# Pooling branch: its gates computed in pairs before the pooling, groups in reverse order, maps one group behind, weight splits by adding DMAs, early products reordered

## The chip, the cores and the metric

The kernel runs on one core of one Trainium2 chip. The metric is the device time of one launch in microseconds (us); three runs before the change gave 894.7, 896.02 and 897.62 us, median 896.02. Engines are named as in the profile: PE (TensorE, matrix products), PEld (its weight loads), DVE (VectorE), ACT (ScalarE), POOL (GpSimd) and SP (SyncE, which issues most DMAs).

## The reference, cut to what matters

One decoder layer on 512 prompt tokens and 64 sample tokens (576 in all), model width 1024, fp32:

```python
xn = rms_norm(h, g_mix[i])
z = xn @ w_in[i]
b, c, hc = z[..., :o1], z[..., o1:o2], z[..., o2:o3]
v = z[..., o3:o4]
gate_a = jax.nn.sigmoid(z[..., o4:o5])
gate_b = jax.nn.sigmoid(z[..., o5:])
ya, cb = gated_short_conv(b, c, hc, conv_bufs[i], w_conv[i])
ya = ya @ w_out_conv[i]
yb, pb = multiscale_pool(v, pool_bufs[i], pos0, w_pool[i], pool_scale[i])
h = h + (gate_a * ya + gate_b * yb) @ w_o[i]
```

`multiscale_pool` takes four groups of 256 channels; in each, the mean over the last 2, 4, 8 or 16 tokens minus the token itself, then a 256x256 map of the group and a scale per channel. A squared-ReLU feed-forward part (1024 to 4096 and back), a per-layer input embedding and a last norm follow. `w_in` has six parts of 1024 output channels: b, c, hc, v, gate a, gate b.

## The kernel before, in words

Channels lie on the 128 partitions, tokens on the free axis in two halves of 288 (256 prompt and 32 sample tokens each). Every fp32 operand of a product is split into a rounded `hi` and a rest `lo` (`split`, L87: ACT writes hi, DVE writes lo = source - hi), and a product is three matmuls per weight block: hi with hi, hi with lo, lo with hi (`mm`, L104). A product of 128 output channels over 1024 input channels (`product`, L118) is 8 x 3 x 2 = 48 matmuls of 288 columns.

Some products are done in pairs of output blocks with a Strassen-like form (`pairs_of`, L416): seven quarter products of 12 matmuls instead of eight, with sums of weights (`Form`, L157, partly added up by DMAs that POOL issues, L154) and sums of activations (`Operand`, L378; `differences`, L407). This is how gate a, most of b's neighbours c and hc, and the feed-forward part's first matrix are computed; gate b and v use plain products. In `pairs_of` a flag `late` holds back the last quarter of the inner index of the first four quarter products.

Weights come through one `Stream` (L180): an ordered list of parts of 128x512, loaded by SP into 8 raw buffers and split some parts ahead into 7 buffers of hi and of lo (`wsp`).

The stages up to the place where the change ends are:
1. Opening: eight input blocks are scaled and split while three plain products (c, hc, b of block 0) run over k = 0 to 7 (L486); the token sums of squares for the norm (`Rms.tokens`, 18 narrow fp32 matmuls, L329) come after k = 5, and the spreading of the norm factors to all partitions (`spread`, L347) after k = 6. `copies` (L352) brings the factors to SBUF as r1 and its square r1s; only then can the products be scaled (L558) and their six PSUM banks be given back.
2. Convolution branch (L553 to L598): block 4 by plain products, then q = 1 to 3 in pairs. The sums of activations for the pairs are made inside the loop over j at L564 to L569.
3. Gate a in pairs (L616), four pairs.
4. The map of the convolution branch, `w_oc` (L630), eight products, multiplied into gate a (`mix`).
5. Pooling (L636 to L694): per group two products of v (L640), running sums on DVE (L657), the pooled difference split (L677), two products for gate b with a sigmoid (L680 to L685), and the group's map (L689) that is scaled, gated and added to mix (L691, L693) and split into `merged`.
6. The output matrix `w_o` (L715): two products are opened together, over the first six blocks of merged first, then the last two (`two_products`, L370).

The compiler's scheduler orders each engine's instructions by priority in program order; where `pinned` is set PE keeps program order (L65).

## Time and profile before

| | |
|---|---|
| median of three runs | 896.02 us |
| the profiled execution | 897.59 us |
| its span, first to last instruction | 895.8 us |
| mean granted TensorE clock, share of full | 0.988 |
| PE busy in the span | 878.8 us, 98% |
| DVE busy | 581.2 us, 65% |
| ACT busy | 405.0 us, 45% |
| POOL busy | 131.1 us, 15% |

PE is busy nearly always, and the chain that ended last runs through it for 94% of the span. Such a busy PE still hides two things: matmuls run at half rate where the granted clock is at the lower of its two levels, and short waits add up. So the reading goes by stages: where PE starts late, how long one matmul takes there, and what it waited for.

### The profile page before, as it was taken

How to read it: one execution, taken by the hardware profiler on the slowest of the kernel's cores; microseconds unless marked ns; L12 is line 12 of the kernel's file. 1: busy time of each engine (PE TensorE's matmuls, PEld its weight loads, DVE VectorE, ACT ScalarE, POOL GpSimd, SP SyncE). 2: the span in 40 equal slices, each digit the busy share in tenths (PEclk: the TensorE clock that was granted, in tenths of full speed). 3: DMA queues.
4: the chain of work that ended last, by engine and by line, in shares of the span. 5: the costliest groups of instructions: out<-in, count | busy, mean ns of one | idle time of the engine just before them, and what ended most of it. 6: DMA issues, size and time to landing. Idle time of an engine off the chain costs nothing.

```text
span 895.8 us, 16709 instructions
## 1 busy us (share of the span) xinstructions
PE 878.8 (98%) x6554; PEld 875.5 (98%) x6554; DVE 581.2 (65%) x1027; ACT 405.0 (45%) x702; POOL 131.1 (15%) x168
## 2 busy tenths in 40 slices
PE   9989999999999999999999999999999999999995
PEld 9979999999999999999999999999999999999995
DVE  7886887985336677767884347534773367687455
ACT  7643443553113333345774237522672157536432
POOL 4101111100001221022110100011000110021354
PEclk9889999999999999999999999999999999999998
DMA  7526455554222222363553535353543544332002
GB/s 258 133 81 145 140 128 149 139 147 140 83 83 83 83 83 83 114 194 92 134 155 104 133 97 137 121 130 101 154 133 87 124 122 130 104 97 94 14 16 91
DMA packets 58125, 103.88 MB, mean 116 GB/s; under 512 B 6848, under 2 KB 10560, under 8 KB 58048
## 3 DMA queue, kind: packets, MB, share of 16 engines
q1 hardware_dynamic: 50416, 89.16, 31.0%
q0 software_dynamic: 7488, 13.63, 9.7%
q8 instruction: 51, 0.84, 0.4%
q14 instruction: 26, 0.21, 0.1%
q10 hardware_dynamic: 144, 0.03, 0.0%
HBM read 99.82 MB, written 2.99 MB: 115 GB/s over the span
## 4 chain that ended last, share of the span: by engine, by line
PE 94%; DVE 3%; DMA 1%; ACT 1%; issue 1%; SPq 0%; DVEq 0%
PE b L67 68%; PE ps L67 18%; PE psg L67 6%; DVE lo L94 1%; PE psn L329 1%; PE psn L347 1%; DMA raw<-w_up 1%; DMA xin<-x 0%; ACT hi L93 0%; DVE xall L808 0%; DVE t L691 0%; DVE gt L409 0%; ACT hi L96 0%; DVE gt L412 0%; DVE gt L411 0%
## 5 line engine op out<-in xcount | busy, mean ns | idle before, releaser
L67 PE MATMUL b<-hi 128*128 128x288 f32 x1592 | 403.1, 298 | 5.2 <-ACT hi L93 3.6
L67 PE MATMUL b<-lo,hi 128*128 128x288 f32 x1592 | 402.1, 297 | 0.7 <-DVE lo L94 0.7
L67 PE MATMUL b<-hi,lo 128*128 128x288 f32 x1592 | 402.1, 297 | 0.4 <-DVE lo L94 0.4
L93 ACT CAST hi<-raw 128x512 fp32r<-128x512 f32 x300 | 184.6, 620 | 323.6 <-PE b L67 214.6
L67 PEld LDWEIGHTS b<-hi 128*128 128x128 f32 x1592 | 278.0, 190 | 6.8 <-ACT hi L93 4.3
L94 DVE TENSOR_TENSOR lo<-raw,hi 128x512 fp32r<-128x512 f32 x300 | 210.6, 707 | 112.0 <-ACT hi L93 108.9
L67 PEld LDWEIGHTS b<-lo,hi 128*128 128x128 f32 x1592 | 278.1, 190 | 1.3 <-DVE lo L94 1.2
L67 PEld LDWEIGHTS b<-hi,lo 128*128 128x128 f32 x1592 | 277.7, 190 | 0.7 <-DVE lo L94 0.7
L67 PE MATMUL ps<-hi 128*128 128x288 f32 x416 | 89.2, 296 | 0.0
L67 PE MATMUL ps<-hi,lo 128*128 128x288 f32 x416 | 89.1, 296 | 0.0
L67 PE MATMUL ps<-lo,hi 128*128 128x288 f32 x416 | 89.1, 296 | 0.0
L154 POOL DMA_DIRECT2D raw<-w_up x32 | 27.7, 865 | 327.6 <-DMA raw<-w_up 188.8
L67 PEld LDWEIGHTS ps<-hi,lo 128*128 128x128 f32 x416 | 67.0, 189 | 0.0
L67 PEld LDWEIGHTS ps<-lo,hi 128*128 128x128 f32 x416 | 67.0, 189 | 0.0
L67 PEld LDWEIGHTS ps<-hi 128*128 128x128 f32 x416 | 67.0, 189 | 0.0
L320 POOL TENSOR_TENSOR sq<-sq 128x576 f32<-128x576 f32 (+2 forms) x32 | 41.2, 1286 | 112.3 <-ACT sq L314 64.6
L174 DVE TENSOR_TENSOR s<-raw 128x512 f32<-128x512 f32 x26 | 17.9, 690 | 49.3 <-DMA raw<-w_up 32.5
L93 ACT CAST hi<-s 128x512 fp32r<-128x512 f32 x52 | 32.0, 617 | 38.1 <-PE b L67 33.0
L94 DVE TENSOR_TENSOR lo<-s,hi 128x512 fp32r<-128x512 f32 x52 | 35.7, 687 | 13.1 <-ACT hi L93 12.1
L67 PE MATMUL psg<-hi 128*128 128x320 f32 (+1 forms) x128 | 38.2, 298 | 0.7 <-ACT r L354 0.7
L67 PE MATMUL psg<-lo,hi 128*128 128x320 f32 (+1 forms) x128 | 37.9, 296 | 0.0
L67 PE MATMUL psg<-hi,lo 128*128 128x320 f32 (+1 forms) x128 | 37.9, 296 | 0.0
(130 smaller groups left out, 751.0 us busy)
## 6 DMA issues: line engine op xcount, KB each, us to landing
raw<-w_in SPq DMA_DIRECT2D x100, 256.0 KB, 2.9
raw<-w_up SPq DMA_DIRECT2D x80, 256.0 KB, 2.9
raw<-w_down SPq DMA_DIRECT2D x64, 256.0 KB, 2.9
raw<-w_up POOLq DMA_DIRECT2D x32, 256.0 KB, 4.4
raw<-w_in POOLq DMA_DIRECT2D x20, 256.0 KB, 4.9
raw<-w_oc SPq DMA_DIRECT2D x16, 256.0 KB, 2.8
raw<-w_o SPq DMA_DIRECT2D x16, 256.0 KB, 2.8
raw<-w_pg SPq DMA_DIRECT2D x16, 256.0 KB, 2.8
```

The source lines that it names most:

```text
L67: i = nc.tensor.matmul(*args, **kw)
L93: nc.scalar.copy(hi, src)
L94: nc.vector.tensor_tensor(out=lo, in0=src, in1=as32(hi), op=ALU.subtract)
L154: nc.gpsimd.dma_start(raw, y, accum_op=ALU.add)
L174: nc.vector.tensor_tensor(out=p.rs2, in0=p.rs1, in1=p.ra, op=ALU.add)
L320: nc.gpsimd.tensor_tensor(out=self.parts[0], in0=self.parts[0], in1=sq, op=ALU.add)
L329: nc.tensor.matmul(sums[:, i:i + 1], a[:, h, c:c + m], ones32[:, 0:1], start=k == 0, stop=k == len(self.parts) - 1)
L347: nc.tensor.matmul(self.ps[:, h, c:c + m], self.y[:, i:i + 1].broadcast_to([m, P]), idt[:m, :m], start=True, stop=True)
```

## The change

Five things are done.

- Opening (L505 and on, new): the sums of squares are issued in three portions of six, each behind one of the three products of k = 5; then the remaining k = 6 and 7 are done product by product, and the spreading is issued in two halves inside the second product.
- Convolution branch: a function `differences(k)` makes the activation sums, called once before the convolution of a block and once before its last product's gate; the first pair (q = 1) uses `late`.
- Gate b is computed in pairs, with the same functions as gate a, after the `w_oc` products and before the pooling. The `w_oc` products come before the scope of pools changes. Gate b's eight tiles live in the `acts` pool.
- Pooling: groups go from window 16 to window 2, a group's map (`merge`) is issued behind the next group's two products, and small copies go from POOL to ACT. The weights of v of the last three groups and of all maps are "adding" parts: ACT writes hi, then lo = -hi, and a DMA issued by POOL adds the weight from HBM onto lo; DVE does not touch them.
- The first two `w_o` products go over merged blocks 2 to 7 first, then 0 and 1, and two PSUM pools change places.

```diff
         def split(self):
+            if self.adding:
+
+                n = self.ap.shape[1]
+                hi = wsp.tile([P, KH], F32R, tag="w", name="hi")[:, :n]
+                lo = wsp.tile([P, KH], F32R, tag="wl", name="lo")[:, :n]
+                nc.scalar.copy(hi, self.raw[:, :n])
+                nc.scalar.mul(lo, as32(hi), -1.0)
+                nc.gpsimd.dma_start(lo, self.ap, accum_op=ALU.add)
+                self.raw = None
+                return hi, lo
...
-    for g in range(4):
+    order += forms([Pair(w_in[5 * NJ + q], w_in[5 * NJ + NQ + q]) for q in range(NQ)])
+    for g in (3, 2, 1, 0, -1):
         for i in range(2):
-            order += unit(w_in[3 * NJ + 2 * g + i])
-        for i in range(2):
-            order += unit(w_in[5 * NJ + 2 * g + i])
-        order += unit(w_pool[g])
+            order += unit(w_in[3 * NJ + 2 * g + i], g < 3) if g >= 0 else []
+        order += unit(w_pool[g + 1], True) if g < 3 else []
...
-    for k in range(NJ):
+    def first_step(k, u):
+        mm(both(ps0[u]), [first[k]], u * P, P, xg[k], k == 0, k == NJ - 1)
+
+    for k in range(NJ - 2):
         for u in range(3):
-            mm(both(ps0[u]), [first[k]], u * P, P, xg[k], k == 0, k == NJ - 1)
-        if k == 5:
-            stat.tokens()
-        if k == 6:
-            r1, r1s = stat.copies(stat.spread(), "r", "rs")
+            first_step(k, u)
+            if k == NJ - 3:
+                stat.sums((2 * u, 2 * u + 1))
+    stat.tokens(summed=True)
+    for u in range(3):
+        for k in (NJ - 2, NJ - 1):
+            first_step(k, u)
+            if u == 1:
+                r = stat.spread(range(3 * (k - NJ + 2), 3 * (k - NJ + 3)))
+    r1, r1s = stat.copies(r, "r", "rs")
...
+        differences(j // 2)
         conv.convolve()
-        conv.gate(ps0[2] if j == 0 else product(stream.take(2), xg))
-        for k in range(j // 2, j // 2 + 2):
-            g = tmp.tile([P, 4, HT], F32, tag="g", name="gx", bufs=2)
-            for i in range(2):
-                nc.scalar.mul(g[:, 2 * i:2 * i + 2], xs[k + i * NQ], v(G_MIX, k + i * NQ))
-            xo.differences(k, g)
+        ps_b = ps0[2] if j == 0 else product(stream.take(2), xg)
+        differences(j // 2 + 1)
+        conv.gate(ps_b)
...
-        pairs_of(2, xo, corner, finish, filler=filler)
+        pairs_of(2, xo, corner, finish, q == 1, filler=filler)
...
+    gates, where, tag = mix, keep, "keep"
+    pairs_of(NQ, xo, corner, finish)
+    for j in range(NJ):
+        ps = product(stream.take(2), ya_in)
+        for h in range(NH):
+            nc.vector.tensor_tensor(out=mix[j][:, h], in0=ps[h], in1=mix[j][:, h], op=ALU.mult)
+    ya_in = None
+    gates, where, tag = [None] * NJ, acts, "act"
     pairs_of(NQ, xo, corner, finish)
...
+    def merge(g, pooled):
+        wp = stream.take()
+        for i in range(2):
+            j = 2 * g + i
+            ps = product(wp, pooled, base=i * P, step=2 * P)
...
+    before = None
+    for g, w in reversed(list(enumerate(WINDOWS))):
...
-        gates = []
-        for i in range(2):
-            ps = product(stream.take(2), xg)
-            z = tmp.tile([P, NH, HT], F32, tag="t", name="zb")
-            nc.vector.tensor_tensor(out=z, in0=halves(ps), in1=r1, op=ALU.mult)
...
+        if before:
+            merge(*before)
+        before = g, pooled
+    merge(*before)
...
-    opened = two_products(merged, range(NJ))
+    opened = two_products(merged, [*range(2, NJ), 0, 1])
```

How the built programs differ is shown at three places. The first is PE in the opening, from the last two products of k = 5 to the spreading; `psn<-ones,sq` are the sums of squares, `psn<-idt,ry` the spreading, and each L67 row is a step of the three products. Before:

```order
L67 MATMUL b<-hi,lo 128x288 x2
L329 MATMUL psn<-ones_121,sq 96x1 x18
L67 MATMUL b<-hi 128x288 x2
...
L67 MATMUL b<-hi,lo 128x288
L347 MATMUL psn<-idt,ry 128x96 x6
L67 MATMUL b<-hi,lo 128x288
L67 MATMUL b<-hi 128x288 x2
```

After:

```order
L340 MATMUL psn<-ones_121,sq 96x1 x6
L67 MATMUL b<-hi 128x288 x2
L67 MATMUL b<-lo,hi 128x288 x2
L67 MATMUL b<-hi,lo 128x288 x2
L340 MATMUL psn<-ones_121,sq 96x1 x6
...
L340 MATMUL psn<-ones_121,sq 96x1 x6
...
L367 MATMUL psn<-idt,ry 128x96 x3
L67 MATMUL b<-hi,lo 128x288
L367 MATMUL psn<-idt,ry 128x96 x3
L67 MATMUL b<-hi 128x288 x2
```

One run of 18 narrow matmuls became three of 6 with six wide matmuls between them (PE runs each fp32 one in two passes, so that the trace shows 36). The spreading stands 23 wide matmuls behind the last sum in both, now in two halves with one wide matmul between, and the whole third product follows it.

The second place is DVE before the first pair of the convolution branch. `gt` and the `lo` made from it are the activation sums of k = 3, `bt` is the gated convolution of block 4, `b` in its source the product it waits for. Before:

```order
L542 TENSOR_TENSOR bt_717<-b_668,r_407 128x288
L94 TENSOR_TENSOR lo_763<-raw_581,hi_762 128x512
L543 TENSOR_TENSOR bt_717<-bt_717,cv_652 128x2x256
L546 TENSOR_TENSOR bt_717<-bt_717,cv_652 128x2x32
L94 TENSOR_TENSOR lo_789<-s2_583,hi_788 128x512
L94 TENSOR_TENSOR lo_723<-bt_717,hi_722 128x576
L94 TENSOR_TENSOR lo_738<-gt_729,hi_737 128x576
L409 TENSOR_TENSOR gt_744<-gx_741 128x576
L411 TENSOR_TENSOR gt_744<-gx_741,gt_744 128x288
L412 TENSOR_TENSOR gt_744<-gx_741,gt_744 128x288
L94 TENSOR_TENSOR lo_749<-gt_744,hi_748 128x576
L94 TENSOR_TENSOR lo_753<-gt_744,hi_752 128x576
```

After:

```order
L429 TENSOR_TENSOR gt_735<-gx_732 128x576
L94 TENSOR_TENSOR lo_757<-raw_522,hi_756 128x512
L431 TENSOR_TENSOR gt_735<-gx_732,gt_735 128x288
L94 TENSOR_TENSOR lo_740<-gt_735,hi_739 128x576
L432 TENSOR_TENSOR gt_735<-gx_732,gt_735 128x288
L570 TENSOR_TENSOR bt_747<-b_682,r_425 128x288
L570 TENSOR_TENSOR bt_747<-b_683,r_425 128x288
L94 TENSOR_TENSOR lo_744<-gt_735,hi_743 128x576
L571 TENSOR_TENSOR bt_747<-bt_747,cv_667 128x2x256
L574 TENSOR_TENSOR bt_747<-bt_747,cv_667 128x2x32
```

The sums of k = 3 stood behind the whole gated convolution; now they stand ahead of it, except for one split.

The third place is PE from the last map of the pooling (group 0, weights `hi_4377`) to the first `w_o` product (`b_4708`), after the change. `hi_4572` and `lo_4573` are the pooled block 1, `hi_4604`/`lo_4605` and `hi_4624`/`lo_4625` are merged blocks 2 and 3, which come from the map issued just before:

```order
L67 MATMUL ps_4654<-hi_4492,lo_4378 128x288 x2
L67 MATMUL ps_4634<-hi_4572,hi_4377 128x288 x2
L67 MATMUL ps_4654<-hi_4572,hi_4377 128x288 x2
L67 MATMUL ps_4634<-lo_4573,hi_4377 128x288 x2
...
L67 MATMUL b_4708<-hi_4604,hi_4424 128x288
...
L67 MATMUL b_4708<-lo_4605,hi_4424 128x288
...
L67 MATMUL b_4708<-hi_4624,hi_4424 128x288
...
L67 MATMUL b_4708<-lo_4625,hi_4424 128x288
...
L67 MATMUL b_4708<-hi_4398,hi_4498 128x288
```

And DVE's own order over the same stretch, after the change (`t` are the merged blocks before their split, `lo_4631` a `w_o` weight):

```order
L94 TENSOR_TENSOR lo_4573<-pl_4566,hi_4572 128x576
L681 TENSOR_TENSOR t_4601<-t_4601,ga_2502 128x576
L681 TENSOR_TENSOR t_4621<-t_4621,ga_2649 128x576
L94 TENSOR_TENSOR lo_4631<-raw_4422,hi_4630 128x512
L94 TENSOR_TENSOR lo_4605<-t_4601,hi_4604 128x576
L679 SCALAR_TENSOR_TENSOR t_4647<-ps_4634,vec_82,ga_3309 128x576
L94 TENSOR_TENSOR lo_4625<-t_4621,hi_4624 128x576
```

Before the change the `w_o` products began with merged blocks 0 to 5, finished two groups earlier; now blocks 2 and 3 come first, right behind the group that makes them.

## Rows read from the trace of the kernel before

**Rows 1.** The page: busy time of each engine in the span, and the chain that ended last by engine.

```profile
PE 878.8 (98%) x6554; PEld 875.5 (98%) x6554; DVE 581.2 (65%) x1027; ACT 405.0 (45%) x702; POOL 131.1 (15%) x168
...
PE 94%; DVE 3%; DMA 1%; ACT 1%; issue 1%; SPq 0%; DVEq 0%
```

**Rows 2.** Busy time in stretches: stretch and its length, then busy us (instructions) of PE, PEld, DVE, ACT and POOL, granted TensorE clock as a share of 2.4 GHz, DMA share, GB/s.

```profile
21.60:25.00 3.40, 3.40 (x38) 3.40 (x36) 2.64 (x5) 1.96 (x2) 0.59 (x1) 0.87 0.75 214
25.00:30.60 5.60, 5.60 (x24) 5.60 (x25) 5.05 (x13) 4.34 (x8) 1.31 (x2) 0.50 0.75 172
...
55.40:60.00 4.60, 1.17 (x5) 0.63 (x4) 4.43 (x8) 2.58 (x5) 0.00 (x0) 0.81 0.17 57
60.00:65.00 5.00, 4.82 (x19) 4.50 (x20) 2.93 (x6) 1.34 (x3) 0.00 (x0) 0.50 0.00 0
...
440.00:454.00 14.00, 12.88 (x97) 12.48 (x96) 11.43 (x18) 9.51 (x17) 4.85 (x4) 1.00 0.56 136
...
821.90:823.00 1.10, 1.10 (x15) 1.10 (x14) 0.77 (x2) 0.76 (x4) 0.00 (x0) 1.00 0.46 168
```

**Rows 3.** PE in order of time in the opening: start, us, engine, line, operation, count, in brackets the idle time before and its releaser.

```profile
21.56 3.55 PE L329 MATMUL psn<-ones,sq 128*96 128x1 f32 x36
...
30.64 1.62 PE L347 MATMUL psn<-idt,ry 96*128 96x96 f32 x12
...
34.09 0.40 PE L67 MATMUL b<-hi 128*128 128x288 f32 x1
```

**Rows 4.** DVE in order of time in the opening and before the first pair, same columns.

```profile
8.09 0.55 DVE L94 TENSOR_TENSOR lo<-fraw,hi 128x384 fp32r<-128x384 f32 x1
...
10.48 1.79 DVE L94 TENSOR_TENSOR lo<-fraw,hi 128x384 fp32r<-128x384 f32 x1
...
27.31 0.15 DVE L340 SCALAR_TENSOR_TENSOR ry<-rz,ry 96x6 f32<-96x6 f32 x1
27.57 0.76 DVE L94 TENSOR_TENSOR lo<-gt,hi 128x576 fp32r<-128x576 f32 x1
...
33.58 0.82 DVE L558 TENSOR_TENSOR c<-b,rs 128x288 f32<-128x288 f32 x2 [2.94 <-ACT rs L358]
...
57.36 0.76 DVE L409 TENSOR_TENSOR gt<-gx 128x576 f32<-128x576 f32 x1
```

**Rows 5.** ACT in order of time, same columns.

```profile
32.29 0.64 ACT L354 COPY r<-psn 128x576 f32<-128x576 f32 x1 [2.48 <-PE psn L347]
32.83 0.66 ACT L358 ACTIVATE rs<-psn 128x576 f32<-128x576 f32 x1
...
59.71 0.39 ACT L421 COPY g<-b 128x288 f32<-128x288 f32 x1
```

**Rows 6.** POOL in order of time, same columns: sums of squares, and the issue of an adding DMA.

```profile
10.11 1.75 POOL L320 TENSOR_TENSOR sq<-sq 128x576 f32<-128x576 f32 x1 [0.17 <-ACT sq L314]
...
17.23 1.89 POOL L320 TENSOR_TENSOR sq<-sq 128x576 f32<-128x576 f32 x1 [1.23 <-ACT sq L314]
...
26.90 0.87 POOL L154 DMA_DIRECT2D raw<-w_in  x1 [1.45 <-DVE rz L339]
```

**Rows 7.** PE in order of time at the first pair of the convolution branch, same columns.

```profile
56.49 0.40 PE L67 MATMUL b<-hi 128*128 128x288 f32 x1 [1.00 <-ACT hi L93]
57.38 0.40 PE L67 MATMUL b<-lo,hi 128*128 128x288 f32 x1 [0.49 <-DVE lo L94]
...
59.86 0.61 PE L67 MATMUL b<-hi 128*128 128x288 f32 x1 [1.95 <-ACT hi L93]
60.65 0.61 PE L67 MATMUL b<-lo,hi 128*128 128x288 f32 x1 [0.18 <-DVE lo L94]
```

**Rows 8.** DVE in order of time in the first pooling group: the pooling of block 1, and gate b's two products read from PSUM (L682).

```profile
273.43 0.69 DVE L645 TENSOR_TENSOR e<-ps,r 128x512 f32<-128x512 f32 x1 [1.46 <-PE ps L67]
...
277.67 0.75 DVE L94 TENSOR_TENSOR lo<-pl,hi 128x576 fp32r<-128x576 f32 x1
279.83 0.76 DVE L682 TENSOR_TENSOR zb<-ps,r 128x576 f32<-128x576 f32 x1 [1.42 <-PE ps L67]
...
286.23 0.76 DVE L682 TENSOR_TENSOR zb<-ps,r 128x576 f32<-128x576 f32 x1 [2.08 <-PE ps L67]
```

**Rows 9.** Busy time in a stretch of gate a's pairs, columns as in rows 2.

```profile
180.00:210.00 30.00, 30.00 (x228) 30.00 (x227) 23.79 (x45) 15.67 (x30) 0.98 (x2) 1.00 0.50 147
```

**Rows 10.** DVE alone in the pooling stage: stretch, its length, busy us (instructions), clock, DMA share, GB/s.

```profile
267.00:380.00 113.00, 82.86 (x143) 1.00 0.27 88
```

**Rows 11.** DVE's groups between 210 and 378 us: line, operation, shapes, count | busy us, mean ns | idle before, releaser.

```profile
L94 DVE TENSOR_TENSOR lo<-raw,hi 128x512 fp32r<-128x512 f32 x53 | 36.3, 686 | 26.3 <-ACT hi L93 26.1
...
L691 DVE SCALAR_TENSOR_TENSOR t<-ps,vec,gb 128x576 f32<-128x576 f32 x8 | 6.5, 818 | 1.3 <-PE ps L67 1.0
...
L693 DVE TENSOR_TENSOR t<-t,ga 128x576 f32<-128x576 f32 x8 | 6.0, 754 | 0.1
```

**Rows 12.** PE in order of time at the end of the pooling, columns as in rows 3.

```profile
376.78 0.53 PE L67 MATMUL b<-hi 128*128 128x288 f32 x2 [0.99 <-DVE t L691]
```

**Rows 13.** The instructions that write or read raw weights: engine, operation, count, duration ns min/median/max, first and last start.

```profile
L93 ACT CAST hi<-raw x300: 600/620/681, 19.5 to 832.3; 128x512 fp32r<-128x512 f32 x150
...
L154 POOL DMA_DIRECT2D raw<-w_in x20: 853/862/1037, 24.4 to 180.9; - x20
```

**Rows 14.** The page's DMA issues: transfer, queue, count, KB each, median us from issue to landing.

```profile
raw<-w_in POOLq DMA_DIRECT2D x20, 256.0 KB, 4.9
```

More of the change, by code (lines that the diff above doesn't have):

```diff
@@ L207, in take, with unit @@
             return out
-    def unit(ap):
-        return [Part(ap[:, i:i + KH]) for i in range(0, ap.shape[1], KH)]
+    def unit(ap, adding=False):
+        return [Part(ap[:, i:i + KH], adding=adding) for i in range(0, ap.shape[1], KH)]
     order = []
@@ L331, in tokens @@
                         start=k == 0, stop=k == len(self.parts) - 1)
+        def tokens(self, pin=False, summed=False):
+            n, m = len(self.at), self.chunk
+            if not summed:
+                self.sums(range(n))
+            sums = self.ps[:m, 0, self.width:self.width + n]
             rt, ms, y, t = (tmp.tile([m, n], F32, tag=g, name=g, bufs=2) for g in ("rt", "ms", "ry", "rz"))
@@ L341, in tokens, with spread @@
             self.y = y
-        def spread(self):
+        def spread(self, pieces=None):
             m = self.chunk
             for i, (h, c) in enumerate(self.at):
+                if pieces is not None and i not in pieces:
+                    continue
                 nc.tensor.matmul(
```

60 lines of the change are left out of this document (28 added, 32 removed).

## The prediction

> **What bounds the kernel now.** I read the page first: PE is busy 98% of the span and carries 94% of the chain that ended last [rows 1]. So the time is the number of matmuls times the time of each, plus PE's few waits, and every other engine matters only where it makes PE wait or where PE's clock is low. Then the stretches by clock, which show where a busy PE is slow: between 25.0 and 30.6 us 24 matmuls take 5.6 us and between 60 and 65 us 19 take 4.8, both at granted clock 0.50, the 1.2 GHz level, while a stretch at 2.4 GHz shows 228 in 30 us [rows 2, 9]. Then PE in order of time just ahead of these two: the narrow sums of squares, 36 passes in about 3.4 us [rows 3], and four waits of 1.00, 0.49, 1.95 and 0.18 us [rows 7]. Last, PE's wait at the end of the pooling, 0.99 us [rows 12]. The profiled execution took 897.59 us, 1.8 more than its span of 895.8 and 1.6 above the median of 896.02; I sum against 897.59 and take 1.6 off at the end.
>
> **The change part by part.**
>
> *Gate b in pairs.* Removed: 8 products of 48 matmuls. One product takes 6.40 us (two reads of gate b from PSUM, at 279.83 and 286.23) [rows 8], so 51.2 us. Added: 4 pairs of 7 quarter products of 12, 336 matmuls; gate a's pairs run at 30/228 = 0.132 us each [rows 9], a few records of a trace may be missing, so I take 0.1325: 44.5 us. That is 6.7 us off PE. With 0.1316 for the pairs it would be 7.0, and with the products' own 6.40/48 = 0.133 for all 48 saved matmuls 6.4. The pairs bring DVE weight sums, rests and corner sums; in gate a's stretch the same work keeps DVE busy 23.8 of 30 us and PE never waits [rows 9], so this hides. If it did not, the whole 6.7 would be gone. The Trainium skill (TensorE: Matmul & The Clock Gate, "Wait — 56ns, not 53.3ns?") gives the columns divided by 2.4 GHz plus 2.5 ns for one matmul: 0.1225 us for 288 columns, by which 48 would be 5.9 us. The rows differ by 8%, and the rows decide.
>
> *Opening.* The number of matmuls is the same, and the order of the sums costs nothing: the last addition of squares on POOL ends at 19.1 us [rows 6], the first portion starts near 20.0 (12 wide matmuls before the 21.56 of now [rows 3]). The norm factors are ready at 27.5 on DVE [rows 4]. Behind the spreading, the path runs in both kernels over two copies on ACT (0.64 and 0.66) and one DVE product to the first free bank, so PE restarts some 1.85 us after the spreading ends (now 34.09 against 32.27) [rows 3, 4, 5]. So this edit is worth only what it does to the clock: 23 or 24 wide matmuls at 0.24 instead of 0.133, 24 x 0.107 = 2.6 us, if the clock no longer falls. Bursts of 12 narrow passes left the clock at 2.4 GHz at 821.9 [rows 2]. But the three bursts of 12 come within 5 us, with only 6 wide matmuls (0.8 us) between two. Nearest to that is the second fall: PE waited 1.00, 0.49 and 1.95 us, worked 0.4 and 0.5 us between, and went on at 1.2 GHz [rows 2, 7]. Short work between did not keep the clock up there, so I forecast that it falls again and that the gain is small: 0.4 us, between 0 and 2.7.
>
> *First pair of the convolution branch.* The waits sum to 3.6 us [rows 7], and between 60 and 65 us 19 matmuls ran where 5.0/0.1325 = 38 would fit, 19 x 0.1325 = 2.5 us [rows 2]: 6.1 us lost. PE waited for the sums of k = 3, made from 57.36 on in a row [rows 4]. They now stand ahead of the gated convolution (second order above), and the matmuls that read them come 36 matmuls later by the late form. DVE's queue from the restart on, by the durations of before: some 40 rows, so the first of these sums is split about 21 us behind the restart, when PE needs it 24 us behind it. They are off the path. What is late next: the copy of the first quarter (0.39 us on ACT [rows 5]) must be read out before PE adds to that bank, and in ACT's queue a weight split of 0.62 us [rows 13] that waits for DVE's weight sum stands ahead of it; I make it 1.1 us of wait, and 0.2 for DVE's corner sums. The same late form in the feed-forward part loses 14.00 - 12.88 = 1.1 us [rows 2]. Net 6.1 - 1.3 = 4.8 us; between 3.0 (another 1.8 of waits) and 6.1.
>
> *Pooling without the gate products beside it.* PE has now 8 products of 6.40 and 4 maps of 24 matmuls (3.2 us), 64 us, as cover for DVE. DVE was busy 82.9 us in this stage [rows 10]. Gate b's reads go (8 x 0.755 = 6.0), and of 35 raw weight splits that I count in the stretch all but 6 of `w_o`'s go to the adding DMAs or to the pairs (29 x 0.686 = 19.9) [rows 8, 11]. 57 of 64 us are left, so DVE keeps up. In the reversed order the long chains (window 16) come first, under the next group's products, and DVE catches up towards window 2. Cost: nothing. Cover: the map of a group waits for work done two products earlier.
>
> *Adding DMAs.* For one part: two ACT operations (0.62 each; the negation is not in the trace of before, taken like the copy), a DMA issue on POOL (0.86) [rows 13], 4.9 us to landing [rows 14], together 7.0 us. A part takes the buffer of the part seven places ahead of it in the list, so between its release and its use lie at least five other parts of 3.2 us, 16 us. Nine us are in hand, behind which POOL's other work in this stage (8 small copies and memsets) and its waits for DVE's buffers fit. Cost nothing; if the landing took three times as long, 14.7, PE would begin to wait.
>
> *End of the pooling.* Now PE waits 0.99 us for a bank [rows 12]; the exchanged pools give the first two `w_o` products banks that are free early, so this goes. Late next are DVE's splits. Let T be the end of the last product. PE needs the pooled block 1 at T + 3.2 + 1.6 = T + 4.8 and its rest 0.5 later. DVE's chain took 4.24 us from its start to the last split [rows 8], one raw split (0.6) leaves it, two scalings of the map before (0.82 each [rows 11]) enter it: its rest ends at 0.2 + 4.24 - 0.6 + 1.6 + 0.75 = T + 6.2 at most. PE loses about 0.7. Then `w_o` begins with blocks 2 and 3, whose sums (0.754 each [rows 11]), a raw split, a scaling and two splits stand in DVE's queue behind that: 4.2 us, the second rest at about T + 10.2. Six matmuls are done by then in this product's first twelve; the twelve end at about T + 10.7 where T + 8.0 would do. So 2.7 us of wait replace 1.0: 1.7 lost. Bounds: 0 if the scheduler's order is kinder, and 4.3 if the clock falls here too (waits of this kind were followed by 1.2 GHz [rows 2, 7]; 2.6 more, as in the opening). I take 2.0.
>
> *Sum:* -6.7 - 0.4 - 4.8 + 2.0 = -9.9 us. 897.6 - 9.9 = 887.7 for an execution like the profiled one, less 1.6: 886.1 us for the median.
>
> **The rivals.**
>
> *The clock stays up in the opening.* For it: no single burst is longer than those that did no harm at 821.9 [rows 2]. Against: [rows 7], where three short waits were enough. The gain is then 2.6 instead of 0.4: 883.9 us. The Trainium skill (TensorE: Matmul & The Clock Gate, "Why this matters for your kernels") warns only of one long idle gap between bursts of matmuls, by which the clock would stay up here. The trace does not agree in rows 7, where it fell behind several short ones.
>
> *The pairs save nothing*, since DVE binds them (its load there is 24 of 30 us [rows 9], and the branch before has left it work). Then 6.7 come back: 892.8 us. Against: gate a shows no wait.
>
> *The pooling stage waits, mildly.* DVE has 7 us to spare of 64; a tenth more on each operation, or weights that land some us late behind POOL's queue, lets PE wait about 5 us: 891 us.
>
> *Slower than before: POOL's DMA issues hold DVE up.* At 10.48 us a split took DVE 1.79 us beside a POOL operation (10.11 to 11.86) where it took 0.55 at 8.09 [rows 4, 6]. If each of 16 adding issues and 8 copies in the pooling stage did that, 24 x 1.24 = 30 us would meet 7 us of room, and PE would wait 23 us: 886 + 23 = 909 us. It makes the change slower as soon as one such meeting costs over 17/24 = 0.7 us. Against: beside the issue at 26.90 to 27.77 DVE's split took 0.76, as usual [rows 4, 6].
>
> **How the numbers follow.** The forecast 0.47 (its own range 884.5 to 888.5), the clock that stays up 0.25, the mild waits 0.12, pairs without gain 0.07, the slower case 0.05, and 0.04 for things not thought of, half of them within the bound. The best ends (7.0, 2.7, 6.1, nothing lost at the end) give 897.6 - 15.8 - 1.6 = 880.2; the range is 881 to 892.5, which holds the first three cases and part of the fourth. A measurement of this kernel tells 0.3%, 2.7 us, from no change: faster is under 893.3, slower over 898.7. Faster 0.88, within it 0.07, slower 0.05.
>
> **What would show it.** PE's records should fall by about 48. The stretch from 25 to 31 us at 0.50 shows the clock's case. From the restart to the next 240 matmuls there should be no wait above about 1.1 us and no low clock. In the pooling stage PE should have no idle time until the last map, then about 2.7 us in four or five pieces that end on DVE `lo` and ACT `hi`. Waits on a DMA for `lo` in that stage, or DVE operations there longer than in rows 11, would make the forecast wrong.

## The result and the profile after

The changed kernel takes 886.97 us (median of 4 executions, 886.27 to 887.5) where the kernel before takes 896.8 beside it: ratio 0.9891, 95% interval 0.9875 to 0.9907, about 9.8 us less. The forecast was 886.1 with a range of 881 to 892.5. The profiled execution took 886.94 us, its span 885.1, 10.7 less than before. Run once more later, it gave 888.03 (6 executions, 887.26 to 889.97; ratio 0.9916, 0.9898 to 0.9935). The ten together have their median at 887.5; what makes them spread over almost 4 us is told below, as far as it is known.

The page of the changed kernel, busy time and chain, as [rows 1]:

```profile
PE 867.9 (98%) x6506; PEld 863.5 (98%) x6506; DVE 594.1 (67%) x1063; ACT 426.5 (48%) x754; POOL 139.5 (16%) x176
...
PE 84%; DVE 9%; issue 3%; DMA 2%; ACT 1%; SPq 0%; POOL 0%; DVEq 0%; POOLq 0%; ACTq 0%
```

PE has the 48 matmuls less that were foretold, and is as busy as before. But the chain that ended last now runs through DVE for 9% instead of 3, some 80 us. 51 of them lie between 305.8 and 362.9 us, in the pooling stage, and most of the rest between 396 and 438 us: there DVE has as little to spare as PE.

Where the 10.7 us came from is read by putting the same points of the two traces side by side:

| point of the program | before | after | gained up to here |
|---|---|---|---|
| PE restarts behind the norm | 34.09 | 31.18 | 2.9 |
| PE starts `w_oc` | 209.25 | 200.44 | 8.8 |
| `w_o`'s products run freely | 376.78 | 362.98 | 13.8 |
| sums of squares in the feed-forward part | 453.91 | 442.55 | 11.4 |
| end of the span | 895.8 | 885.1 | 10.7 |

So the opening gave 2.9 us, the first pair 5.9, the gates and the pooling together 5.0, and 2.4 were lost again between `w_o` and the feed-forward part, in a place of which the prediction had said nothing. The last 0.7 is net: behind 852.4 us (864.7 before) 1.7 us were lost, where the clock fell a little earlier, and 1.0 was gained in the 42 us ahead of that.

*Opening and first pair.* Stretches of the changed kernel, columns as in [rows 2]:

```profile
24.00:26.00 2.00, 2.00 (x19) 2.00 (x19) 1.17 (x6) 1.83 (x5) 1.04 (x1) 1.00 0.58 159
26.00:28.00 2.00, 2.00 (x18) 2.00 (x17) 1.89 (x6) 2.00 (x5) 0.87 (x1) 1.00 0.84 145
...
60.00:65.00 5.00, 5.00 (x39) 4.84 (x38) 5.00 (x11) 2.16 (x4) 0.86 (x1) 1.00 0.59 156
```

The granted clock is 1.00 in both places where [rows 2] showed 0.50. PE in order of time in the opening, as [rows 3]:

```profile
19.96 1.10 PE L340 MATMUL psn<-ones,sq 128*96 128x1 f32 x12
...
21.79 1.10 PE L340 MATMUL psn<-ones,sq 128*96 128x1 f32 x12
...
23.63 1.10 PE L340 MATMUL psn<-ones,sq 128*96 128x1 f32 x12
...
31.18 0.40 PE L67 MATMUL b<-hi 128*128 128x288 f32 x1 [0.21 <-DVE c L592]
```

Three bursts of 12 passes, 0.7 us of wide matmuls between them, and the clock stayed up in this execution. The forecast had said the opposite.

*End of the pooling.* PE in order of time, as [rows 12]:

```profile
361.01 0.40 PE L67 MATMUL b<-hi 128*128 128x288 f32 x1
362.98 0.41 PE L67 MATMUL b<-hi 128*128 128x288 f32 x1 [1.56 <-DVE t L679]
```

and DVE just before the second of these:

```profile
362.11 0.81 DVE L679 SCALAR_TENSOR_TENSOR t<-ps,vec,ga 128x576 f32<-128x576 f32 x1
```

`w_o`'s very first matmul runs at 361.01, the second stands 1.56 us. It has the same weights and the other half of the tokens, so what it misses is its bank: DVE reads block 0's product out of it until 362.92. With three short losses in front of it (0.8 us in all from 358.4 on) PE lost 2.7 us there, counted from the starts of its matmuls at 0.1325 us each. That is the forecast's 2.7; by the same count the kernel before lost 1.3 at this place, where the forecast took its 0.99.

*The new loss.* DVE in order of time in `w_o`'s stretch, after:

```profile
395.88 0.69 DVE L184 TENSOR_TENSOR s<-raw 128x512 f32<-128x512 f32 x1 [5.59 <-DMA raw<-w_up]
...
416.78 0.82 DVE L755 TENSOR_TENSOR xall<-b,xall 128x288 f32<-128x288 f32 x2
```

and the same two instructions before:

```profile
407.10 0.69 DVE L174 TENSOR_TENSOR s<-raw 128x512 f32<-128x512 f32 x1 [3.13 <-DMA raw<-w_up]
...
428.15 0.82 DVE L719 TENSOR_TENSOR xall<-b,xall 128x288 f32<-128x288 f32 x2
```

L184 adds two weights of the feed-forward part's second pair, and stands idle until the adding DMA of that pair has landed; `w_o`'s sums are queued behind it. Counted from the point where `w_o` runs freely (362.98 here, 376.78 before), its wait ends 32.9 us behind it, before it was 30.3. By that the last sums of `w_o` (L755) come 2.4 us later, and PE waits for what is made from them:

```profile
419.96 0.40 PE L67 MATMUL b<-lo,hi 128*128 128x288 f32 x1 [0.40 <-DVE lo L94]
...
421.37 0.40 PE L67 MATMUL b<-lo,hi 128*128 128x288 f32 x1 [0.75 <-DVE lo L94]
...
422.74 0.40 PE L67 MATMUL b<-hi 128*128 128x288 f32 x1 [0.45 <-ACT g L441]
```

### The profile page after: what moved, and what is told of

Read it like the earlier page. It is cut to its first block, busy times and chain, and to the rows that moved or that the text cites. A ratio compares the mean times of both kernels' runs of the same rounds, so it can differ in the third digit from the quotient of the medians.

```text
span 885.1 us, 16776 instructions
## 1 busy us (share of the span) xinstructions
PE 867.9 (98%) x6506; PEld 863.5 (98%) x6506; DVE 594.1 (67%) x1063; ACT 426.5 (48%) x754; POOL 139.5 (16%) x176
## 4 chain that ended last, share of the span: by engine, by line
PE 84%; DVE 9%; issue 3%; DMA 2%; ACT 1%; SPq 0%; POOL 0%; DVEq 0%; POOLq 0%; ACTq 0%
PE b L67 76%; PE psg L67 6%; DVE lo L94 2%; DVE q L706 2%; DMA raw<-w_up 2%; PE psn L340 1%; DMA xin<-x 1%; PE psn L367 1%; ACT hi L93 1%; DVE pl L710 1%; DVE t L679 1%; DVE e L694 0%; DVE t L681 0%; PE ps L67 0%; DVE xall L755 0%
## 5 line engine op out<-in xcount | busy, mean ns | idle before, releaser
L67 PE MATMUL b<-hi 128*128 128x288 f32 x1832 | 461.9, 296 | 4.3 <-DVE t L679 1.6
L67 PE MATMUL b<-lo,hi 128*128 128x288 f32 x1832 | 460.4, 295 | 1.2 <-DVE lo L94 1.1
L67 PE MATMUL b<-hi,lo 128*128 128x288 f32 x1832 | 460.6, 295 | 0.6 <-DVE lo L94 0.6
L67 PEld LDWEIGHTS b<-hi 128*128 128x128 f32 x1832 | 317.6, 188 | 6.7 <-DVE t L679 1.8
L67 PEld LDWEIGHTS b<-lo,hi 128*128 128x128 f32 x1832 | 317.6, 188 | 1.8 <-DVE lo L94 1.6
L67 PEld LDWEIGHTS b<-hi,lo 128*128 128x128 f32 x1832 | 317.5, 188 | 0.9 <-DVE lo L94 0.8
L184 DVE TENSOR_TENSOR s<-raw 128x512 f32<-128x512 f32 x30 | 20.7, 690 | 45.5 <-DMA raw<-w_up 28.9
L67 PE MATMUL psg<-hi 128*128 128x320 f32 (+1 forms) x128 | 38.1, 298 | 0.0
L67 PE MATMUL psg<-lo,hi 128*128 128x320 f32 (+1 forms) x128 | 37.9, 296 | 0.0
L67 PE MATMUL psg<-hi,lo 128*128 128x320 f32 (+1 forms) x128 | 37.9, 296 | 0.0
L67 PE MATMUL ps<-lo,hi 128*128 128x288 f32 x160 | 34.4, 296 | 0.0
L67 PE MATMUL ps<-hi 128*128 128x288 f32 x160 | 34.2, 296 | 0.1
L67 PE MATMUL ps<-hi,lo 128*128 128x288 f32 x160 | 34.2, 296 | 0.0
L94 DVE TENSOR_TENSOR lo<-g,hi 128x576 fp32r<-128x576 f32 x32 | 26.3, 834 | 6.6 <-ACT hi L93 6.6
```

Source lines behind the costliest of these rows:

```text
L67: i = nc.tensor.matmul(*args, **kw)
L94: nc.vector.tensor_tensor(out=lo, in0=src, in1=as32(hi), op=ALU.subtract)
L184: nc.vector.tensor_tensor(out=p.rs2, in0=p.rs1, in1=p.ra, op=ALU.add)
```

## The experiments

All are the changed kernel with one edit, or with the two or three that are named, 4 to 9 executions each, beside the kernel before on the same chip; the numbers compared are the ratios to it. The changed kernel stands at 0.9891 and 0.9916, and 0.0010 is 0.9 us.

**The opening put back.**

```diff
-            if k == NJ - 3:
-                stat.sums((2 * u, 2 * u + 1))
...
+        if k == 5:
+            stat.tokens()
+        if k == 6:
+            r1, r1s = stat.copies(stat.spread(), "r", "rs")
```

> The changed kernel with only the opening put back: the six sums of squares in one run of 36 narrow matmuls behind the sixth block, the spreading behind the seventh. Theory (the clock): the changed kernel's opening saves what the granted clock of 0.50 had cost. With the old order PE's first wide matmul behind the norm comes at about 34.1 us of the span instead of 31.2, the windows between 25 and 31 us show a granted clock of 0.50 again, and the time is 886.97 + 2.9 = about 889.9 us. Rival 1 (what the prediction took): the order is worth only 0.4 us, so about 887.4. Rival 2: the 2.9 us come back later, because a later wait ends at a fixed time: restart at 34.1, but the time within 0.5 us of 887.

Ratio 0.9922 (0.9902 to 0.9943), 888.34 us: 2.8 us slower than the first ratio of the changed kernel, 0.5 slower than the second, with intervals that overlap; the times alone do not show a loss. Stretches of its trace:

```profile
24.00:26.00 2.00, 2.00 (x15) 2.00 (x15) 1.33 (x8) 1.99 (x5) 1.04 (x1) 0.83 0.42 135
26.00:28.00 2.00, 2.00 (x10) 2.00 (x9) 1.90 (x5) 2.00 (x4) 0.87 (x1) 0.50 0.96 146
28.00:30.00 2.00, 2.00 (x17) 2.00 (x16) 1.87 (x4) 0.62 (x2) 0.00 (x0) 0.81 0.82 215
```

The clock falls again, for 3.4 us where it was 6.8 before, and PE restarts at 32.06 instead of 31.18. The theory has its direction, not its size.

**The three bursts in one run, nothing else moved.**

```diff
-            if k == NJ - 3:
-                stat.sums((2 * u, 2 * u + 1))
+        if k == NJ - 3:
+            stat.sums(range(6))
```

> The changed kernel with the three bursts of 12 narrow matmuls joined to one run of 36, at the same block (behind the sixth) and with everything behind it as in the changed kernel. Theory (the length of the narrow run sets the clock): the granted clock falls to 0.50 behind the run, the wide matmuls that follow take 0.24 us instead of 0.133, and PE's restart comes 2.6 us later, at about 33.8: 889.6 us. Rival (the fall of before came from the wait for the norm, or the place of the run, not from its length): the clock stays at 1.00 and the time within 0.5 us of 887.

Ratio 0.9913 (0.9898 to 0.9929), 888.32 us (886.41 to 889.68). Its profile:

```profile
24.00:26.00 2.00, 2.00 (x12) 2.00 (x12) 0.74 (x6) 1.40 (x4) 1.04 (x1) 0.50 0.42 143
26.00:28.00 2.00, 2.00 (x10) 2.00 (x10) 1.90 (x5) 2.00 (x5) 0.87 (x1) 0.50 0.83 135
```

10 matmuls in 2 us where the changed kernel has 18, and the restart at 34.00, 2.8 us later, as the theory has it. But the executions do not lie 2.6 us higher: they cover the same 886.4 to 889.7 us as the changed kernel's, so the times show no loss.

**The first pair put back.**

```diff
-        differences(j // 2)
         conv.convolve()
-        ps_b = ps0[2] if j == 0 else product(stream.take(2), xg)
-        differences(j // 2 + 1)
-        conv.gate(ps_b)
+        conv.gate(ps0[2] if j == 0 else product(stream.take(2), xg))
+        for k in range(j // 2, j // 2 + 2):
+            differences(k)
...
-        pairs_of(2, xo, corner, finish, q == 1, filler=filler)
+        pairs_of(2, xo, corner, finish, filler=filler)
```

> The changed kernel with the first pair of the convolution branch put back: the differences of k = 1 and 3 behind the gate as before, and no late form for the first pair. Theory: the whole loss of before comes back, waits of 3.6 us and a granted clock of 0.50 in a 5 us stretch (2.5 us), against 0.6 us of waits in the changed kernel: the products of w_oc start at about 206.3 instead of 200.4, and the time is 887 + 5.9 = 892.9 us. By the term on record it would be 887 + 4.8 = 891.8. Rival: the opening's clock was the cause of this loss too (the pair came after a slow start), so that without it the old order loses only about 1 to 2 us: 888.5.

Ratio 0.9963 (0.9951 to 0.9976), 892.84 us: 4.2 to 6.5 us slower. PE in order of time at the pair, as [rows 7]:

```profile
55.46 0.40 PE L67 MATMUL b<-hi 128*128 128x288 f32 x1 [0.99 <-ACT hi L93]
56.35 0.40 PE L67 MATMUL b<-lo,hi 128*128 128x288 f32 x1 [0.49 <-DVE lo L94]
...
58.83 0.40 PE L67 MATMUL b<-hi 128*128 128x288 f32 x1 [1.95 <-ACT hi L93]
```

These three waits of before are back, within a hundredth, and the granted clock is 0.50 again from 59.2 to 62.6 us. From PE's restart to the start of `w_oc` the trace takes 174.95 us, the changed kernel 169.26: 5.7 us that do not depend on the opening. In its own opening, though, where it has the changed kernel's code, the clock fell this time:

```profile
24.00:26.00 2.00, 2.00 (x16) 2.00 (x16) 1.17 (x6) 1.84 (x5) 1.04 (x1) 0.75 0.40 138
26.00:28.00 2.00, 2.00 (x10) 2.00 (x10) 1.91 (x6) 2.00 (x4) 0.87 (x1) 0.50 0.89 140
```

Whether the early sums or the late form alone would do was not tried.

**Gates as plain products, at the new place.**

```diff
-    order += forms([Pair(w_in[5 * NJ + q], w_in[5 * NJ + NQ + q]) for q in range(NQ)])
+    for j in range(NJ):
+        order += unit(w_in[5 * NJ + j])
...
-    pairs_of(NQ, xo, corner, finish)
+    for j in range(NJ):
+        ps = product(stream.take(2), xg)
...
```

> The changed kernel with the pooling branch's gates as 8 plain products of 48 matmuls, at their new place ahead of the pooling. Theory: 384 matmuls replace 336, 51.2 us stand where 44.75 stood, so 887 + 6.45 = 893.4 us; the stage behind is the same, with its waits at the end (2.4 us). Rival: the pairs' extra work on DVE is what makes the pooling stage start with a backlog and end late; then the products would give back some of the 2.4 us, and the time is 891 to 892.

Ratio 0.9952 (0.9938 to 0.9966), 891.89 us: 3.2 to 5.5 slower, less than the 6.45 us that the pairs take off PE. It is the time that the rival named (891 to 892), but not for its reason: the bank's wait of 1.56 us at the pooling's end is there in both. The gates take 51.2 us in this trace and 44.6 in the changed kernel's, so the pairs do save their 6.6 us. From `w_o`'s first matmul to the sums of squares in the feed-forward part it needs 79.2 us, the changed kernel 81.5. That these 2.3 us are a cost of the pairs is not shown: the kernel with the first pair put back keeps the gates in pairs, and its DVE waits 3.48 us for the summed weight, as here (3.40), not 5.59, and PE has no wait in the 70 us behind the bank's. The edit also moves something else:

```profile
L673 SPq DMA_DIRECT2D sp<-spool x1: 382/382/382, 204.9 to 204.9; - x1
```

The load of the pooling's state is issued beside `w_oc`, and DVE does not wait for it; what this load does in the changed kernel is told further down.

**The changed kernel again.**

> The changed kernel itself once more, on the same chip and beside the same runs of the kernel before as the three that follow, with a second profile of its opening. Two runs with this very opening (the first pair undone, the gates as products) showed the granted clock at 0.50 between 24 and 30 us, where the changed kernel's own profile showed 1.00. Theory (chance): the three bursts of 12 narrow matmuls leave the clock up in some executions only, so the times spread over some 2.6 us, from 886 to 889. Rival (the two other profiles were disturbed): the clock is 1.00 between 20 and 34 us again and the times stay within 886.3 to 887.5.

The times were 887.26 to 889.97. In its profile the opening's clock is 1.00, but this stands at the end of the pooling, PE first:

```profile
361.05 0.80 PE L67 MATMUL ps<-hi 128*128 128x288 f32 x4 [2.58 <-ACT hi L93]
...
365.18 0.61 PE L67 MATMUL b<-hi 128*128 128x288 f32 x1 [0.81 <-DVE t L679]
```

then the stretches there:

```profile
362.00:364.00 2.00, 2.00 (x9) 2.00 (x9) 2.00 (x4) 0.94 (x2) 0.00 (x0) 0.50 0.00 0
364.00:366.00 2.00, 1.19 (x5) 0.84 (x5) 2.00 (x4) 0.93 (x2) 0.00 (x0) 0.50 0.41 125
```

So executions of one kernel differ, in more than one place, and why is not known. In ten profiles with the three bursts (the kernels below included) the clock fell in the opening in three; at the pooling's end it fell here and in two others, which the prediction had kept as its bound of 4.3 us. The falls in the opening moved PE's restart by 1.4 to 3.0 us.

**The narrow sums strewn one by one.**

```diff
+        if narrow:
+            narrow.pop(0)()
...
+        if k == NJ - 3:
+            narrow.extend(stat.sums(range(6)))
```

> The changed kernel with the 18 narrow sums strewn one by one behind the 18 wide matmuls of the sixth block instead of in three bursts; their number, and the matmuls behind them, stay. Theory 1 (it is the length of a narrow burst that lets the clock fall): the clock stays at 1.00 in every execution, the spreading starts at about 27.7 us as in the best profile, and the time is 886.5 to 887 with a spread under 1 us. Theory 2 (it is the share of narrow work in these 5 us, however it is mixed): the clock falls in as many executions as with the bursts, granted clock 0.50 between 24 and 30 us, 887 to 889.

Ratio 0.992 (0.9902 to 0.9938), 888.94 us (887.42 to 889.72), no gain, and not the spread of under 1 us that was expected. The one profile has a clock of 1.00 through the opening and the spreading at 27.94. Nothing can be said from it against the bursts; whether mixing helps stays open.

**The order of blocks in `w_o`'s opening, and with it the halves apart.**

```diff
-    opened = two_products(merged, [*range(2, NJ), 0, 1])
+    opened = two_products(merged, [6, 7, 4, 5, 2, 3, 0, 1])
```

> The changed kernel with the first two products of w_o starting with the blocks that are ready first (6, 7, 4, 5, 2, 3, 0, 1 instead of 2 to 7, 0, 1). Theory (a bank): the wait of 1.56 us at 362.98 is the second half's bank, which the product of block 0 holds until DVE has read it at 362.92; the order of the blocks doesn't touch that, so the wait stays and the time changes by under 0.5 us: 887. Rival (the term on record): PE waits for the splits of blocks 2 and 3, which now come later in the order; the waits at the end of the pooling fall from 2.4 to under 1 us and the time is about 885.4.

Ratio 0.9926 (0.9901 to 0.9951), 888.91 us. PE in its trace:

```profile
363.10 0.40 PE L67 MATMUL b<-hi 128*128 128x288 f32 x1 [1.89 <-DVE t L679]
```

The wait is where it was, though the blocks that it could have been waiting for come last now. It is the bank. The second edit lets PE write that bank later:

```diff
-                steps(ps, w, operands, part, first=ks[0], last=ks[-1])
+                for outs in ([[o] for o in both(ps)] if apart else [both(ps)]):
+                    for k in part:
+                        mm(outs, w, k * P, P, operands[k], k == ks[0], k == ks[-1])
...
+    opened = two_products(merged, [6, 7, 4, 5, 2, 3, 0, 1], True)
```

> The same order of blocks, and the two opening products of w_o take one half of the tokens after the other (18 matmuls into the first bank, then 18 into the second), so that PE writes the second bank 2.4 us later. Theory (a bank): the wait of 1.56 us goes and none takes its place at the end of the pooling; w_o's first matmul still comes at about 361.0 behind the last map, and w_o ends 1.9 us earlier. The feed-forward part then loses as much as before or more, since DVE there waits for the landing of a summed weight: between 885 and 887. Rival: DVE is late anyhow, and the wait reappears at the blocks 2 and 3: no gain, 887.

Ratio 0.9914 (0.9893 to 0.9934), 887.84 us. PE in order of time:

```profile
363.08 0.40 PE L67 MATMUL b<-lo,hi 128*128 128x288 f32 x1 [0.57 <-DVE lo L94]
...
420.36 0.40 PE L67 MATMUL b<-hi 128*128 128x288 f32 x1 [2.05 <-ACT hi L93]
```

The bank's wait is gone, and what it gave was lost again 57 us later, where the clock fell as well. But the halves did not bring that loss. The kernel with the order of blocks alone has it too, with its clock down from 423.1 us on:

```profile
421.91 0.40 PE L67 MATMUL b<-hi 128*128 128x288 f32 x1 [2.04 <-ACT hi L93]
```

In both kernels DVE waited for two summed weights of the feed-forward part (9.7 and 10.7 us in all) instead of one; no other profile with these adding DMAs shows that.

**Plain loads for the summed weight, in the first two pairs of the feed-forward part.**

```diff
-                p.rs1 = p.summed(p.c, p.d)
+                if getattr(p, "plain", False):
+                    p.rs1, p.rd1 = raw_tile(p.c), raw_tile(p.d)
...
+                    nc.vector.tensor_tensor(out=p.rs1, in0=p.rs1, in1=p.rd1, op=ALU.add)
...
+        ups[0].plain = ups[1].plain = b == 0
```

> The changed kernel, where the first summed weight of the first two pairs of the feed-forward part comes by two plain loads and an addition on DVE (0.68 us each) instead of a load and an adding DMA behind it. Theory (the landing of that DMA): in the changed kernel DVE stood idle 5.6 us for it at 395.88 (3.1 in the kernel before) with the sums of w_o's rows queued behind, which made PE lose 4.8 us at w_o's end and in the first pair instead of 2.3. With the plain loads that idle time falls under 2.5 us, the last additions of w_o come within 1 us of w_o's last matmul, and PE's losses there fall to about 2.3: 884.5 to 885.5 where the changed kernel has 887 to 888. Rival (DVE's weight splits behind buffers that PE frees late): DVE waits there for ACT's splits instead, and the time is the changed kernel's.

Ratio 0.9879 (0.9857 to 0.99), 885.35 us (882.82 to 886.46). DVE's waits for these weights in `w_o`'s stretch (who waits for what: us in all, times, the longest):

```profile
DVE raw L188 <- DMA raw<-w_up: 2.2, 2, 1.5
```

From `w_o`'s first matmul to the sums of squares it now takes 78.96 us (81.54 before the edit), and the three waits of 420 to 423 us are gone. In the opening of this profiled execution the clock fell, and it was still faster than the changed kernel's best. The intervals of the ratios overlap; it is the trace that shows what the edit does.

**Plain loads and halves apart together.** Both edits above.

> The same plain loads together with the blocks' order and the halves one after the other in the opening of w_o. Theory: each of the two alone passes its gain on to the other's wait; together both waits go, w_o starts at 361 without a bank wait and the first pair behind it waits under 1.5 us in all, so that the granted clock stays at 1.00 from 360 to 430 us: 883 to 884.5 us. Rival: w_o's rows are bound by DVE's queue whatever feeds it, and the first pair of the feed-forward part loses what w_o's opening gains: 886 to 888.

Ratio 0.9866 (0.9844 to 0.9888), 883.74 us. No stretch from 360 to 430 us has a low clock. But a wait of 2.25 us stands at the last map, like the one that the changed kernel showed in its second profile. What DVE did 50 us earlier tells why; PE first, then DVE:

```profile
360.34 0.79 PE L67 MATMUL ps<-hi 128*128 128x288 f32 x4 [2.25 <-ACT hi L93]
```

```profile
307.31 0.22 DVE L706 TENSOR_TENSOR e<-ps,r 128x64 f32<-128x64 f32 x1 [4.49 <-POOL e L702]
```

In the changed kernel's two profiles the same row reads, first and second:

```profile
305.83 0.23 DVE L697 TENSOR_TENSOR e<-ps,r 128x64 f32<-128x64 f32 x1 [2.31 <-POOL e L693]
```

```profile
308.03 0.23 DVE L697 TENSOR_TENSOR e<-ps,r 128x64 f32<-128x64 f32 x1 [4.83 <-POOL e L693]
```

POOL copies the pooling's state `sp` there, and waits for its load, in the changed kernel's first profile so:

```profile
305.51 0.29 POOL L693 COPY e<-sp 128x120 f32<-128x120 f32 x1 [3.71 <-DMA sp<-spool]
```

From the stage's first matmul to `w_o`'s first one it took 64.77 us with the 2.31 and 68.00 with the 4.83.

**Low parts by DVE again instead of adding DMAs.**

```diff
-            self.ap, self.resident, self.adding = ap, resident, adding
+            self.ap, self.resident, self.adding = ap, resident, False
```

> The changed kernel with the low parts of the pooling stage's weights made by DVE again (subtractions of 0.69 us) instead of adding DMAs. Theory: 13 parts less 8 of the first group's are split by adding DMAs, 16 in all with the pooling weights; DVE has 55.4 of 64 us to do and gets 16 x 0.69 = 11.0 more, 66.4 of 64, so it runs behind and PE waits at the end of the pooling some 3 to 6 us longer than now: 890 to 893. Rival (DVE's load does not decide there, as the waits come from the order at the end): under 0.5 us.

Ratio 0.9904 (0.9882 to 0.9927), 886.54 us: the changed kernel's time within the noise, as the rival had it, but not for its reason. One stretch of the pooling stage, the changed kernel and this one, columns as in [rows 2]:

```profile
300.00:364.00 64.00, 62.32 (x461) 61.40 (x461) 55.44 (x102) 31.26 (x62) 16.28 (x28) 1.00 0.70 160
```

```profile
300.00:364.00 64.00, 61.53 (x456) 60.60 (x455) 60.25 (x114) 23.79 (x49) 5.79 (x15) 1.00 0.29 93
```

DVE has 12 instructions and 4.8 us more to do, not the 11.0 us that I had written for all 16 parts. At the same time the DMA engines are busy 29% instead of 70, and DVE's wait for the state is 0.57 us instead of 2.31 or 4.83. The state's load landed in 5.5 us; in the ten profiles with adding DMAs and this load in the same place it took 7.0 to 10.3. So the adding DMAs take work off DVE and make it wait for the state; that the two cancel is a reading of this one profile, in which the clock also fell at the pooling's end and at the start of the feed-forward part, for 3.4 us each.

**The state loaded early.** The halves, the plain loads, and:

```diff
+    sp = []
+    for i in range(2):
+        t = acts.tile([P, NH, HT], F32, tag="act", name="sp")
...
+        nc.sync.dma_start(t, spool[:, i * NQ:(i + 1) * NQ])
...
-    nc.sync.dma_start(sp, spool)
```

> The last kernel (halves apart, plain loads) with the pooling's state loaded ahead of w_oc into two buffers of its own, some 80 us before its use, where the changed kernel issues this load (480 KB) at 297.8 us, at the start of the pooling stage, among its weights. Theory (the state's landing): in the traces so far DVE waited 0.6 to 4.8 us at about 306 for the state's copy on POOL, behind this load, and from there on DVE has next to no idle time until the last map; where it waited 4.5 or more, PE waited 2.2 to 2.6 us at the last map (358 us), where it waited under 3.2, at most 0.9. With the state there early, DVE's wait goes, PE's wait at the last map goes, from the stage's first matmul to w_o's first one it is 64.0 to 64.5 us (66.75 in the profile of the last kernel), and the time is 881 to 883 us, the spread smaller. Rival (the stage's end is set by DVE's own chain of operations, the load's landing is hidden): the wait at 358 us stays at about 2 us and the time at 883.7.

Ratio 0.9844 (0.9825 to 0.9863), 882.40 us (881.01 to 883.86): faster than the changed kernel, the intervals lie apart, and the fastest version of this study. Its DVE goes from the first read of the stage to the next group's work without the wait:

```profile
302.86 0.69 DVE L708 TENSOR_TENSOR e<-ps,r 128x512 f32<-128x512 f32 x1 [5.35 <-PE ps L67]
303.47 0.21 DVE L711 TENSOR_TENSOR e<-ps,r 128x64 f32<-128x64 f32 x1
...
309.29 0.76 DVE L94 TENSOR_TENSOR lo<-pl,hi 128x576 fp32r<-128x576 f32 x1 [0.74 <-ACT hi L93]
```

The stage takes 64.46 us up to `w_o`'s first matmul, no wait at the last map is left, and the clock stays at 1.00 up to the tail. Against the kernel without this last edit the times alone don't prove it (0.9866 against 0.9844, intervals that overlap), and one trace could be a lucky one. The profiles of the other runs bear it out. Where the state is loaded in the stage and the adding DMAs are in place, the longer DVE waits for the state, the longer PE waits at the last map:

| DVE's wait for the state, us | 1.65 | 1.94 | 2.31 | 2.57 | 2.71 | 3.11 | 4.49 | 4.63 | 4.83 | 4.90 |
|---|---|---|---|---|---|---|---|---|---|---|
| PE's wait at the last map, us | under 0.1 | under 0.1 | under 0.1 | 0.35 | 0.46 | 0.86 | 2.25 | 2.39 | 2.58 | 2.63 |

About 2.2 us are taken up on the way, and what is beyond them reaches PE in full. The two profiles with the state loaded early, this one and that of the gates as plain products, show neither wait.

## Why the prediction was right, and where not

*Gate b in pairs, -6.7:* right. The pairs stand from about 251.6 to 296.25, 44.6 us for the 44.5 that were worked out, in place of 51.2. The experiment gives only 3.2 to 5.5 of the time; the kernel that it is compared with loses time behind the gates, in some executions, to the late state and the late summed weight. That the pairs are to blame is shown for the state's load alone, which they hold back.

*Opening, -0.4:* wrong in its step "I forecast that it falls again". It did not in the profiled execution, and in seven of the ten profiles with the bursts it did not; with one long run it fell in three of three. In the profile the term was worth 2.9, the rival's 2.6 and a little more. The times of the two experiments do not tell its worth from nothing. An estimate from the traces: PE's restart comes at 31.8 us in the mean of the ten profiles with bursts and at 33.4 in the mean of the three with one run, so the edit is worth about 1.5 us, between the forecast and the rival, and what I should have written is a share of falls, not a yes or no. The Trainium skill (TensorE: Matmul & The Clock Gate, "Part 1: The HAM clock gate") says that the number of matmuls that one kernel runs at the low clock at its start differs from run to run; the traces here show the like at a later point, with restarts from 30.9 to 34.2 us behind one and the same opening.

*First pair, -4.8:* right in its mechanism and some 1.1 us too small. Put back it costs 4.2 to 6.5 us by the times and 5.7 by the trace. The waits that I had put in its place (1.1 for the copy, 0.2 for the corner sums) came to some 0.5 in all, so that by its own sum the term would be 6.1 - 0.5 = 5.6; the trace shows 5.9.

*The pooling without the gate products beside it, 0:* mis-argued. DVE's load was right, 55.4 of 64 us for the 57 worked out, but the step "so DVE keeps up" counted only DVE's work. The load of the state had been issued at 211 us, beside `w_oc`; now the gate pairs stand between, in the memory that the stage's buffers take over, and it is issued at 297.8, when it is wanted:

```profile
L627 SPq DMA_DIRECT2D sp<-spool x1: 384/384/384, 211.2 to 211.2; - x1
```

```profile
L667 SPq DMA_DIRECT2D sp<-spool x1: 412/412/412, 297.8 to 297.8; - x1
```

(before, then after: line, operation, duration ns, first and last start). It took 7.7 us to land among the weights. Of the 7 to 9 us that DVE had in hand, 2.3 to 4.8 went there in the two profiles of this kernel; the table above shows that only about 2.2 could be spared. In the second profile this is the "mild waits" rival, 2.6 us of its 5, with another cause. A load that has to move with its stage was to be counted in the sum, and it was not.

*Adding DMAs, 0:* right by its number. Neither side of what they do was seen, the 4.8 us of DVE and the later landing of the state; that these cancel is argued from one profile.

*End of the pooling, +2.0:* right by its size (2.7 us lost for 2.7, in place of 1.3), wrong in a step: "the exchanged pools give the first two `w_o` products banks that are free early" holds for one of the first product's two banks. The order of the blocks, on which I had spent the sum, does not decide that wait: with another order it was 1.89 us. (By its own figures the pooled block's rest, at T + 6.2 against T + 5.3, costs 0.9 and not 0.7; the 2.7 does not rest on it.)

*Not foreseen, +2.4:* the loss in front of the feed-forward part. Its cause is shown by the plain loads: DVE's wait for an adding DMA, with DVE's queue behind it. Why the DMA landed late is not settled. Of the 2.6 us in the first profile 1.4 are a slower landing (5.9 us instead of 4.5) and 1.2 a later issue. In the second profile it landed in 4.1 us, faster than before, and DVE still waited:

```profile
398.88 0.69 DVE L184 TENSOR_TENSOR s<-raw 128x512 f32<-128x512 f32 x1 [4.64 <-DMA raw<-w_up]
```

There all of it is the later issue, 29.6 us behind the point where `w_o` runs freely for 25.8 before. Slow landings often had a plain load of the same size issued 0.4 to 0.5 us after them, but not always: with such a load 1.0 us behind it the DMA took 5.7 us in one profile and 4.4 in another. Crowding was not tried by itself.

So the sum was right in part by luck: the opening gave 2.5 and the first pair 1.1 us more than foretold, and 2.4 and 0.7 were lost where nothing was. Profile against profile the sum fell 0.8 us short (887.7 against 886.94 us); the 1.6 us taken off for the median, which the changed kernel's profiled execution did not differ from, turned that into 0.9 the other way. The slower side ("POOL's DMA issues hold DVE up", 909 us) did not come: no DVE operation took over 0.95 us between 290 and 363 us, the whole pooling stage, whatever POOL issued beside it.

## What to carry to other kernels

When a block of work is moved ahead of a stage, look for the loads of that stage that were hidden beside it: they move with the buffers they need, and arrive when they are wanted. An engine with a tenth of its time to spare can pass a late landing on to the end of its stage: here the first 2.2 us were taken up and the rest reached PE in full. Such waits are found one by one: with the summed weight's gone the median was 885.4 us, with the bank's and then the state's gone too 883.7 and 882.4, from 887.5. And a single profile of a kernel whose clock falls by chance is one draw: a few profiles are cheap beside an explanation of 2.6 us that the next one doesn't show.

## What was not expected of the hardware

- The same opening code left TensorE at 2.4 GHz in seven profiles and let it fall to 1.2 in three, for 3.4 us in one and 6.8 in two, with the same instructions ahead of it.
- A low clock also came at the end of the pooling and at the start of the feed-forward part, in three profiles each, behind waits of 0.4 to 2.6 us; the changed kernel's first profile went through both places at 1.00, with waits of 1.56 and of 0.40, 0.75 and 0.45 us, and the kernel with the strewn sums through the first one with 2.39 and 1.56.
- An adding DMA of 256 KB landed in 4.1 to 5.9 us at the same place of the program, and the state's load of 480 KB in 7.0 to 10.3 us at another, where it took 3.6 to 3.8 beside `w_oc`. What else was on the way is the likely cause, and was not tried by itself.
